# Gated linear attention on one core: the head norms' factors placed among the weight splits, the second scaling one unit later, the first scaled queries in other tiles

## The chip, the cores and the metric

The kernel runs on one core of one Trainium2 chip. The metric is the time of one execution on the device, in microseconds; the median of the runs shown counts. The kernel before takes 2088.75 us (median of 3 runs, 2087.92 to 2089.33).

## What is computed

One layer of a streaming encoder over 256 frames of width 2048, in float32: half a SwiGLU, a mixer, a cross attention over 256 memory tokens, another half SwiGLU, and a norm. The change lies in the mixer. One projection `W_in` gives a pool group, and queries, keys, values and an output gate for four heads of gated linear attention. Cut to what matters:

```python
qc = q * DK ** -0.5;  k_dec = k * exp(b_end - cum);  q_dec = qc * exp(b_end)
scores = einsum(qc, k_dec);  o = einsum(scores, v) + einsum(q_dec, state)   # chunks of 64 frames
o = o * rsqrt(mean(o * o, axis=-1) + 1e-6)        # a norm of its own for every head
o = o * head_norm * silu(g)                       # g: the output gate's projection
x = x + concat(y_pool, o) @ W_out
```

The kernel folds the decay between chunks into copies of the queries that are scaled by products of decays, one set per head: these are the scaled queries. The factor of a head norm is one number per frame and head.

## The kernel before, in words

**Weights and units.** The work is a stream of units. A unit is 1 MB of weights in a `raw` tile, loaded by SyncE, and the TensorE products that use it. For float32 accuracy ScalarE casts a rounded high part (`wh`, line 1621) and VectorE subtracts it to get the low part (`wl`, line 453); these two are the weights' parts. Some units save products by adding blocks first (a tile `T` at line 486, parts `xh` and `xl` at lines 279 and 280). There are three buffers each of `raw`, `wh` and `wl`, and parts are made up to two units ahead of the products.

**Order.** `st.op(f, after)` places a step `f` so many units later in the stream. What the program issues is then ordered, engine by engine, by a scheduler that works with a timeline of its own. Two helpers bind it: the parts of the weights follow one another on ScalarE and on VectorE (`in_turn`, line 257), and `among_weights` (line 270) places a step behind the parts issued so far on both engines and makes the next parts follow the last instruction that the step returns. A step outside these helpers goes where the scheduler finds room, instruction by instruction.

**The mixer.** The order of its blocks in `W_in` is: queries and keys, the low-rank gate, values, two pool blocks (`block_a`, products at line 347 into `pa`), the output gate (`block_s`, lines 362 and 507, into `pt`), with the pool map among it. The attention runs between these products. `decay` (line 1067) makes the decays `E` and their products `F`. `scores(h)` copies and scales the queries of head `h` (lines 1152 and 1154), multiplies them with the keys (line 1162) and moves the result to `ST` (line 1168). `attend` multiplies with the values (lines 1175 and 1178) and squares the result (line 1184). `head_norms(b)` does the following for heads 2b and 2b+1: it sums the squares on TensorE into `pn` (line 1197), takes the factor with `rsqrt` (lines 209 to 224: five VectorE instructions on 128x4 values with a ScalarE square root at line 215 behind the first), and makes four diagonal tiles from it (`diagonal`, line 228). `head_scale(b)` multiplies ones with the diagonals on TensorE (line 233, `ps`) to spread the factors, and multiplies the heads' output `oz` with them (line 1211). `gate` (line 1218) uses that result after the output gate's block.

The end of the attention falls into the second pool block, which has four units (parts `wh_6023`, `wh_6103` and `wh_6173` are its last three), and into the first units of the output gate (`wh_6231`, then the tile that holds `raw_6107`, then the unit of `raw_6177`, which adds blocks first).

Of the kernel before, what the change touches and what calls it, by code (L numbers as in the profile page):

```python
# [7 lines left out]
F32 = mybir.dt.float32  # L8
# [6 lines left out]
P = 128  # L15
# [5 lines left out]
NB = 512  # L21
# [3 lines left out]
DV = 256  # L25
# [74 lines left out]
def build(ctx, tc, I, out):  # L100
# [9 lines left out]
    scope = {"stack": None}  # L110
# [26 lines left out]
    def ptile(name):  # L137
        return psum.tile([P, 2, NB], F32, tag="ps", name=name)
# [6 lines left out]
    def uid(s):  # L145
        cnt[0] += 1
        return f"{s}{cnt[0]}"
# [61 lines left out]
    def rsqrt(dst, sums, n, w):  # L209

        v, r = chain[:, 0, :w], chain[:, 1, :w]
        nc.vector.tensor_scalar(
            out=v, in0=sums, scalar1=0.25 / n, scalar2=0.25 * EPS, op0=ALU.mult, op1=ALU.add
        )
        nc.scalar.activation(r, v, AF.Sqrt)
        nc.vector.reciprocal(out=dst, in_=r)
        if w == 1:
            nc.vector.tensor_scalar(
                out=v, in0=v, scalar1=dst, scalar2=r, op0=ALU.mult, op1=ALU.add
            )  # L220
        else:
            nc.vector.tensor_tensor(out=v, in0=v, in1=dst, op=ALU.mult)
            nc.vector.tensor_tensor(out=v, in0=v, in1=r, op=ALU.add)
        return nc.vector.reciprocal(out=dst, in_=v)

    def diagonal(col):
        d = scope["pool"].tile([P, P], F32, tag="diag", name=uid("diag"), bufs=4)
        nc.vector.tensor_scalar_mul(d, ident, col)
        return d
# [35 lines left out]
    def behind_weights(f):  # L265

        with tc.issue_after(latest["vector"].ins), tc.issue_after(latest["scalar"].ins):
            return f()

    def among_weights(f):  # L270


        scalar, vector = behind_weights(f)
        latest["vector"] = vector
        if scalar is not None:
            latest["scalar"] = scalar
# [682 lines left out]
    def mt(name, shape, tag=None, bufs=1):  # L959
        t = whole_lines(scope["pool"], shape, F32, tag or name, uid(name), bufs)  # L960
        mix[name] = t
        return t
# [12 lines left out]
    def m4():  # L975
        return scope["pool"].tile([P, 2 * 2 * (S + PAD)], F32, tag="m4", name=uid("m4"), bufs=3)
# [155 lines left out]
    def score_tile(h):  # L1132
        if h < 2:
            s = ctile() if h else mt("ST", [P, 2, S], "wa2")
        else:
            if h == 2:
                mix["two"] = scope["pool"].tile([P, 4 * NB], F32, tag="T", name=uid("ST"), bufs=1)
            s = mix["two"][:, (h - 2) * NB : (h - 1) * NB].rearrange("p (a b) -> p a b", a=2)
        mix["ST", h] = s
        nc.gpsimd.memset(s[64:128, 0, 0:CH], 0.0)  # L1140
        nc.gpsimd.memset(s[64:128, 1, 2 * CH : 3 * CH], 0.0)
        return s

    def scores(h):
        q, kd, E, F = mix["q"][:, h, :], mix["k"][:, h, :], mix["E"], mix["F"]
        e = lambda c: E[:, 4 * h + c : 4 * h + c + 1]
        f = lambda i: F[:, i, h : h + 1]
        QD = scope["pool"].tile([P, 3 * NB], F32, tag=("xh", "xl")[h % 2], name=uid("QD"), bufs=1)
        at = (0, 3 * CH, 5 * CH)
        factors = {(0, 1): e(1), (0, 2): f(0), (0, 3): f(2), (1, 2): e(2), (1, 3): f(1), (2, 3): e(3)}  # L1150
        for j in range(3):
            nc.scalar.copy(QD[:, at[j] + j * CH : at[j] + (j + 1) * CH], q[:, j * CH : (j + 1) * CH])
            for c in range(j + 1, 4):
                nc.vector.tensor_scalar_mul(
                    QD[:, at[j] + c * CH : at[j] + (c + 1) * CH], q[:, c * CH : (c + 1) * CH],
                    factors[j, c],
                )
        ps = ptile(uid("pq"))
        for j in range(4):
            part = slice((j % 2) * CH, (j % 2 + 1) * CH)  # L1160
            rhs = QD[:, at[j] + j * CH : at[j] + S] if j < 3 else q[:, 3 * CH :]
            nc.tensor.matmul(
                ps[part, j // 2, j * CH : S], kd[:, j * CH : (j + 1) * CH], rhs, start=True, stop=True
            )
        s = score_tile(h)
        for j in range(4):
            part = slice((j % 2) * CH, (j % 2 + 1) * CH)
            nc.vector.tensor_copy(s[part, j // 2, j * CH :], ps[part, j // 2, j * CH : S])
# [23 lines left out]
    def head_norms(b):  # L1192
        pn = ptile(uid("pn"))
        for i in range(2):
            sq = mix["osq", 2 * b + i]
            for t in range(2):
                nc.tensor.matmul(
                    pn[:, 0, 2 * i + t : 2 * i + t + 1], sq[:, 0, t * P : (t + 1) * P],
                    ones[:, 0:1], start=True, stop=True,
                )  # L1200
        r = mt("r", [P, 4])
        rsqrt(r, pn[:, 0, :4], DV, 4)
        mix["diag"] = [diagonal(r[:, i : i + 1]) for i in range(4)]

    def head_scale(b):
# [38 lines left out]
    for f, h, after in (  # L1244
        (scores, 0, 1), (scores, 1, 1), (scores, 2, 2), (scores, 3, 2), (head, 0, 3), (head, 1, 3),
        (head_norms, 0, 4), (head, 2, 4), (head_scale, 0, 5), (head, 3, 5), (head_norms, 1, 6),
        (head_scale, 1, 7),
    ):
        st.op(lambda f=f, h=h: f(h), after)
    block_a(wblock(w_in, 0), xs, ev_pool(0))  # L1250
# [166 lines left out]
    for b in range(2):  # L1417
# [3 lines left out]
        for j in (1, 0):  # L1421
            h = 2 * b + j
# [218 lines left out]
def program(shapes):  # L1641
    import concourse.bacc as _bacc

    nc = _bacc.Bacc("TRN2", target_bir_lowering=False, num_devices=1)
    args = {
        name: nc.dram_tensor(f"in_{name}", shapes[name], F32, kind="ExternalInput").ap()
        for name in _INS
    }
    out = nc.dram_tensor("out", _OUT, F32, kind="ExternalOutput").ap()
    with tile.TileContext(nc, schedule_with_timeline_sim=True) as tc, ExitStack() as ctx:  # L1650
        build(ctx, tc, args, out)
    return nc
# [10 lines left out]
```

## Time and profile before

| | us |
|---|---|
| median of 3 runs | 2088.75 |
| the profiled execution, by the clock of the runs | 2088.16 |
| its span, first to last instruction | 2086.4 |
| TensorE matmul busy | 2065.4 |
| VectorE busy | 1840.4 |
| ScalarE busy | 1157.2 |

The span leaves out 1.8 us that lie around it. A row of the timeline gives the start in us from the span's start, the duration in us, the engine (PE is TensorE, DVE VectorE, ACT ScalarE, SP SyncE), line, operation and tiles, how many instructions are merged in it, and in brackets the idle time before it with what ended that. Matmuls overlap, so a start-to-start distance says more than a duration. A row of the waits gives the total in us, the number of times and the longest. A row of the windows gives the busy time and count of each engine in a stretch, and PEclk, the share of the full TensorE clock that was granted.

### The profile page before, as it was taken

What the parts mean: (1) busy time and instruction counts of PE and PEld (TensorE: products, weight loads), DVE (VectorE), ACT (ScalarE), POOL (GpSimd) and SP (SyncE); (2) the same over time, 40 slices, a digit from 0 to 9 for tenths busy, and PEclk for the clock granted to TensorE, in tenths of its full rate; (3) what the DMA queues carried; (4) which work ended last, traced back from release to release, by engine and by line L of the source; (5) the groups of instructions that cost most, each with busy time, mean ns of one, the idle gap of its engine ahead of it and who ended that gap; (6) DMA issues with size and microseconds to landing.
All of it is one profiled execution on the core that took longest, in us unless ns stands there. A gap on an engine that the chain in (4) does not pass through costs nothing.

```text
span 2086.4 us, 24196 instructions
## 1 busy us (share of the span) xinstructions
PE 2065.4 (99%) x9531; PEld 1719.8 (82%) x9531; DVE 1840.4 (88%) x1745; ACT 1157.2 (55%) x1157; POOL 107.5 (5%) x98
## 2 busy tenths in 40 slices
PE   9999999999999999899999999999999999999998
PEld 7888888888888888788888888888888888888886
DVE  7998899989998768779888887889988999889987
ACT  7655455645554665365756544566554556545554
POOL 0000000000000000000001000000100010000001
PEclk9999999999999999999999999999999999999999
DMA  7666666567656655366855555666576765676664
GB/s 263 207 200 229 231 222 222 182 224 243 222 198 224 231 175 182 121 202 222 278 186 179 169 187 175 207 206 228 183 237 209 240 205 198 223 242 222 207 229 150
DMA packets 125034, 435.94 MB, mean 209 GB/s; under 512 B 9844, under 2 KB 13528, under 8 KB 124536
## 3 DMA queue, kind: packets, MB, share of 16 engines
q1 hardware_dynamic: 124744, 433.86, 61.6%
q8 instruction: 75, 1.23, 0.2%
q10 hardware_dynamic: 176, 0.53, 0.1%
q14 instruction: 39, 0.32, 0.0%
HBM read 417.58 MB, written 16.78 MB: 208 GB/s over the span
## 4 chain that ended last, share of the span: by engine, by line
PE 97%; DVE 1%; issue 0%; ACT 0%; DMA 0%; SPq 0%; DVEq 0%; ACTq 0%
PE pt L362 61%; PE pt L507 29%; PE pa L347 2%; PE ph L782 1%; PE pl L1357 1%; PE pv L1394 1%; DVE wl L453 0%; PE px L793 0%; PE pp L1027 0%; DMA x<-in_x 0%; PE pe L362 0%; ACT wh L1621 0%; PE pa L1054 0%; PE po L1175 0%; PE tm L1304 0%
## 5 line engine op out<-in xcount | busy, mean ns | idle before, releaser
L362 PE MATMUL pt<-wh,xs 128*128 128x512 f32 x2368 | 761.4, 391 | 0.3 <-ACT xs L236 0.3
L453 DVE TENSOR_TENSOR wl<-raw,wh 128x2048 fp32r<-128x2048 f32 (+1 forms) x245 | 521.5, 2136 | 100.3 <-ACT wh L1621 100.0
L1621 ACT CAST wh<-raw 128x2048 fp32r<-128x2048 f32 x245 | 467.6, 1912 | 244.4 <-PE pt L362 122.0
L362 PEld LDWEIGHTS pt<-wh,xs 128*128 128x128 f32 x2368 | 444.9, 188 | 92.2 <-ACT xs L236 0.5
L489 ACT CAST wh<-T 128x1024 fp32r<-128x1024 f32 x258 | 270.6, 1054 | 377.5 <-DVE T L486 363.4
L362 PE MATMUL pt<-wl,xs 128*128 128x512 f32 x1184 | 462.5, 391 | 0.0
L362 PE MATMUL pt<-wh,ys 128*128 128x512 f32 x1440 | 454.8, 389 | 0.0
L362 PEld LDWEIGHTS pt<-wh,ys 128*128 128x128 f32 x1440 | 270.2, 188 | 55.6
L453 DVE TENSOR_TENSOR wl<-T,wh 128x2048 fp32r<-128x2048 f32 (+1 forms) x129 | 289.8, 2246 | 3.0 <-ACT wh L489 2.4
L362 PE MATMUL pt<-wl,ys 128*128 128x512 f32 x720 | 280.8, 390 | 0.6 <-DVE wl L453 0.6
L362 PEld LDWEIGHTS pt<-wl,xs 128*128 128x128 f32 x1184 | 222.9, 188 | 45.4 <-DVE wl L280 0.2
L280 DVE TENSOR_TENSOR xl<-raw,xh 128x1536 fp32r<-128x1536 f32 x129 | 225.8, 1751 | 17.8 <-ACT xh L279 17.7
L279 ACT CAST xh<-raw 128x1536 fp32r<-128x1536 f32 x129 | 190.9, 1480 | 65.8 <-PE pt L507 43.4
L486 DVE TENSOR_TENSOR T<-T,raw 128x512 f32<-128x512 f32 x258 | 177.9, 690 | 6.7
L362 PEld LDWEIGHTS pt<-wl,ys 128*128 128x128 f32 x720 | 135.2, 188 | 28.9 <-DVE wl L453 1.0
L457 POOL TENSOR_TENSOR wl<-raw,wh 128x768 fp32r<-128x768 f32 x46 | 85.4, 1857 | 1421.0 <-DVE wl L453 1394.8
L486 DVE TENSOR_TENSOR T<-raw 128x1024 f32<-128x1024 f32 x129 | 157.0, 1217 | 0.5
L507 PE MATMUL pt<-wh,xs 128*128 128x512 f32 x388 | 150.8, 389 | 0.0
L507 PE MATMUL pt<-xh,xs 128*128 128x512 f32 x400 | 149.1, 389 | 0.0
L507 PE MATMUL pt<-wh,xe 128*128 128x512 f32 x320 | 124.3, 389 | 0.0
L507 PEld LDWEIGHTS pt<-xh,xs 128*128 128x128 f32 x400 | 75.1, 188 | 15.6
L507 PEld LDWEIGHTS pt<-wh,xs 128*128 128x128 f32 x388 | 72.8, 188 | 15.1
(257 smaller groups left out, 2184.9 us busy)
## 6 DMA issues: line engine op xcount, KB each, us to landing
raw<-in_ffn_w_down SPq DMA_DIRECT2D x88, 1024.0 KB, 5.4
raw<-in_ffn_w_up SPq DMA_DIRECT2D x80, 1024.0 KB, 5.0
raw<-in_ffn_w_gate SPq DMA_DIRECT2D x77, 1024.0 KB, 5.1
raw<-in_w_in SPq DMA_DIRECT2D x32, 1024.0 KB, 5.1
raw<-in_xattn_w_kv SPq DMA_DIRECT2D x32, 1024.0 KB, 5.0
raw<-in_w_out SPq DMA_DIRECT2D x16, 1024.0 KB, 5.6
raw<-in_xattn_w_q SPq DMA_DIRECT2D x16, 1024.0 KB, 5.7
raw<-in_xattn_w_o SPq DMA_DIRECT2D x16, 1024.0 KB, 5.7
```

The costliest lines, as they stand in the source:

```text
L279: in_turn("scalar", lambda: nc.scalar.copy(hi, src))
L280: in_turn("vector", lambda: nc.vector.tensor_tensor(out=lo, in0=src, in1=f32(hi), op=ALU.subtract))
L347: nc.tensor.matmul(o, w, x, start=k == 0 and i == 0, stop=last and i == 1)
L362: nc.tensor.matmul(ps, a, w, start=first and i == 0, stop=last and i == 2)
L453: in_turn("vector", lambda: nc.vector.tensor_tensor(out=lo[:, :n], in0=src[:, :n], in1=f32(hi[:, :n]), op=ALU.subtract))
L457: rest = nc.gpsimd.tensor_tensor(out=lo[:, n:], in0=src[:, n:], in1=f32(hi[:, n:]), op=ALU.subtract)
L486: in_turn("vector", lambda: nc.vector.tensor_tensor(out=o, in0=a, in1=b, op=ALU.add))
L489: in_turn("scalar", lambda: nc.scalar.copy(th[:, c], t[:, c]))
L507: nc.tensor.matmul(banks[n], x, w, start=n in fresh and j == 0, stop=n in ends and j == 2)
L782: nc.tensor.transpose(v[:, i, h * P : (h + 1) * P], g[:, h, i * P : (i + 1) * P], ident)
L1357: nc.tensor.matmul(ps[:, t, :M], ys[:, 4 * h + d, a, tok], xa["K", h][:, d, b, :], start=i == 0, stop=i == 11,)
L1621: in_turn("scalar", lambda: nc.scalar.copy(hi, raw))
```

## The change

Three edits, all in the mixer:

```diff
 def scores(h):
-        QD = scope["pool"].tile([P, 3 * NB], F32, tag=("xh", "xl")[h % 2], name=uid("QD"), bufs=1)
+        QD = m4() if h < 2 else scope["pool"].tile(
+            [P, 3 * NB], F32, tag=("xh", "xl")[h % 2], name=uid("QD"), bufs=1
+        )
...
 def head_norms(b):
         r = mt("r", [P, 4])
-        rsqrt(r, pn[:, 0, :4], DV, 4)
+        among_weights(lambda: (None, rsqrt(r, pn[:, 0, :4], DV, 4)))
...
         (head_norms, 0, 4), (head, 2, 4), (head_scale, 0, 5), (head, 3, 5), (head_norms, 1, 6),
-        (head_scale, 1, 7),
+        (head_scale, 1, 8),
```

The scaled queries of heads 0 and 1 get tiles of the tag `m4` (three buffers, used by the decay and the pool blocks) and no longer the `xh` and `xl` tiles that the parts of the weights use. The factor's steps become one group among the weights' parts; the diagonals stay outside it. The scaling of the second pair is issued one unit later. From line 1149 on, line numbers grow by two.

**VectorE at the end of the second pool block, before.** `pn_6211` holds the sums of squares of the second pair, `r_6216` its factor, `diag_6223` the first of its diagonals; line 212, which reads `pn_6211`, stands three rows above the first one shown.

```order
L216 RECIPROCAL r_6216<-chain 128x4
L486 TENSOR_TENSOR T_6329<-T_6329,raw_6177 128x512
L280 TENSOR_TENSOR xl_6333<-raw_6177,xh_6332 128x1536
L323 TENSOR_TENSOR m_6314<-m_6314,R_5413 128x2x256
L222 TENSOR_TENSOR chain<-chain,r_6216 128x4
L453 TENSOR_TENSOR wl_6331<-T_6329,wh_6330 128x2048
L997 TENSOR_TENSOR m_6315<-m_6314 128x2x271
L223 TENSOR_TENSOR chain<-chain 128x4
L997 TENSOR_TENSOR m_6316<-m_6315 128x2x269
L224 RECIPROCAL r_6216<-chain 128x4
L997 TENSOR_TENSOR m_6315<-m_6316 128x2x265
L228 TENSOR_SCALAR diag_6223<-ident,r_6216 128x128
```

The factor's small steps stand between sums, parts of weights and the pool's windows. The parts `wl_6232` and `wl_6277` of the gate's first two units stand ahead of all of this.

The same place after the change, from the last head's output on:

```order
L1192 TENSOR_TENSOR t_6155<-t_6155 128x256
L212 TENSOR_SCALAR chain<-pn_6211 128x4
L216 RECIPROCAL r_6216<-chain 128x4
L222 TENSOR_TENSOR chain<-chain,r_6216 128x4
L223 TENSOR_TENSOR chain<-chain 128x4
L224 RECIPROCAL r_6216<-chain 128x4
L453 TENSOR_TENSOR wl_6232<-raw_6026,wh_6231 128x2048
L453 TENSOR_TENSOR wl_6270<-raw_6107,wh_6269 128x2048
L486 TENSOR_TENSOR T_6329<-raw_6177 128x1024
L228 TENSOR_SCALAR diag_6223<-ident,r_6216 128x128
```

The five steps now follow one another; the parts of the gate's first two units and one sum have moved from ahead of them to between the factor and its diagonals.

On ScalarE at that place, after the change (`wh_6269` is the high part that was `wh_6276`; `c_6318` and `c_6374` are copies out of the pool block's accumulators):

```order
L1186 ACTIVATE t_6155<-po_6150 128x512
L1623 CAST wh_6269<-raw_6107 128x2048
L279 CAST xh_6332<-raw_6177 128x1536
L215 ACTIVATE chain<-chain 128x4
L318 COPY c_6318<-pa_6109 128x512
L318 COPY c_6374<-pa_6110 128x512
```

Before, the square root at line 215 stood one row lower, behind the copy `c_6318`; it is still behind both casts.

**TensorE at the same place, after the change.**

```order
L347 MATMUL pa_6110<-xs,wl_6174 128x256
L347 MATMUL pa_6110<-xs,wh_6173 128x512
L233 MATMUL ps_6307<-diag_6223,ones 128x128
L362 MATMUL pt_6344<-wh_6231,xs 128x512
L362 MATMUL pt_6344<-wl_6232,xs 128x512
```

Although the scaling is issued a unit later, the first of its four spreads stays between the pool block's last product and the gate's first one, as before, and the other three stay sixteen matmuls later. The second matmul into `pn_6211` (from `t_6155`) has moved from the middle of the block's last unit to the end of the unit before.

**VectorE at the first scaled queries** (`m_5840` and `m_5862` are the tiles of heads 0 and 1, `T_5662` and `xl_5666` belong to the unit of `raw_5538`, one of the last of the values' block), as a piece of the difference:

```order
 L1101 TENSOR_TENSOR F_5589<-E_5584 128x4
+L1156 TENSOR_SCALAR m_5840<-q_5523,E_5584 128x64 x3
 L486 TENSOR_TENSOR T_5662<-T_5662,raw_5538 128x512
+L1156 TENSOR_SCALAR m_5862<-q_5523,E_5584 128x64 x2
 L1102 TENSOR_TENSOR F_5589<-F_5589,E_5584 128x4
+L1156 TENSOR_SCALAR m_5840<-q_5523,F_5589 128x64 x2
+L1156 TENSOR_SCALAR m_5862<-q_5523,F_5589 128x64 x2
+L1156 TENSOR_SCALAR m_5862<-q_5523,E_5584 128x64
```

With two more, twelve scalings move ahead of the last low parts of the values' block (`xl_5666`, `wl_5664`, `wl_5701`); on ScalarE their six copies move ahead of `xh_5665` and `wh_5663` in the same way. The scalings of heads 2 and 3 take the room in which those of heads 0 and 1 stood, and leave theirs in the first pool block.

## The prediction

> **What bounds the kernel now.** I read the page first: the busy times and the chain that ended last.
>
> ```profile
> span 2086.4 us, 24196 instructions
> PE 2065.4 (99%) x9531; PEld 1719.8 (82%) x9531; DVE 1840.4 (88%) x1745; ACT 1157.2 (55%) x1157; POOL 107.5 (5%) x98
> PE 97%; DVE 1%; issue 0%; ACT 0%; DMA 0%; SPq 0%; DVEq 0%; ACTq 0%
> ```
>
> TensorE is busy for 99% of the span and is 97% of the chain. The change adds no product and takes none away, so it can only touch the time in which TensorE stands still or runs slowly. The waits of TensorE, the second view, say how much that is.
>
> ```profile
> PE ps L233 <- DVE diag L228: 8.3, 1, 8.3
> PE pwarm L206 <- POOL ident masks.py:199: 1.4, 1, 1.4
> PE px L719 <- DMA x<-in_x: 1.0, 1, 1.0
> PE pt L362 <- DVE wl L453: 0.6, 1, 0.6
> ```
>
> One wait is worth more than all the others together: the first spread of a head norm's factor waits 8.3 us for its diagonal. The timeline of TensorE puts it at the end of the second pool block, so it is the second pair's (the view counts one wait, so the first pair's had none).
>
> ```profile
> 857.62 0.39 PE L347 MATMUL pa<-xs,wh 128*128 128x512 f32 x1
> 866.35 0.77 PE L233 MATMUL ps<-diag,ones 128*128 128x128 f32 x2 [8.34 <-DVE diag L228]
> ```
>
> The last pool product ends at 858.0 and the spread starts at 866.35. The wait also has an aftermath, which the windows show, on the columns PE busy (count) and PEclk.
>
> ```profile
> core 0: us, PE busy (x) PEld busy (x) DVE busy (x) ACT busy (x) POOL busy (x), PEclk, DMA share, GB/s
> 858.00:861.00 3.00, 0.01 (x1) 0.00 (x0) 3.00 (x6) 2.52 (x4) 0.00 (x0) 1.00 0.79 306
> 861.10:866.30 5.20, 0.00 (x0) 0.00 (x0) 5.20 (x10) 0.00 (x0) 0.14 (x1) 0.50 0.61 203
> 866.40:871.20 4.80, 4.80 (x13) 3.83 (x14) 4.63 (x11) 0.62 (x1) 0.00 (x0) 0.50 0.00 0
> 871.40:876.20 4.80, 4.80 (x25) 4.01 (x25) 3.67 (x7) 1.42 (x2) 0.00 (x0) 1.00 0.00 0
> ```
>
> About 3 us into the wait the granted clock falls to one half, and it stays there for some 4.8 us of work: 13 matmuls where the next 4.80 us hold 25. That costs 12/25 of 4.80, or 2.3 us. Wait and aftermath together are 10.6 us, 0.5% of the time, and no edit here can win more.
>
> **The factor's chain, step by step.** Before, VectorE was late because other work stood between the steps of the factor.
>
> ```profile
> 853.88 2.29 DVE L453 TENSOR_TENSOR wl<-raw,wh 128x2048 fp32r<-128x2048 f32 x1 [3.61 <-ACT wh L1621]
> 856.10 1.22 DVE L486 TENSOR_TENSOR T<-raw 128x1024 f32<-128x1024 f32 x1
> 857.23 0.15 DVE L212 TENSOR_SCALAR chain<-pn 128x4 f32<-128x4 f32 x1
> ...
> 858.59 0.17 DVE L216 RECIPROCAL r<-chain 128x4 f32<-128x4 f32 x1
> ...
> 861.52 0.15 DVE L222 TENSOR_TENSOR chain<-chain,r 128x4 f32<-128x4 f32 x1
> ...
> 864.43 0.15 DVE L223 TENSOR_TENSOR chain<-chain 128x4 f32<-128x4 f32 x1
> ...
> 865.18 0.17 DVE L224 RECIPROCAL r<-chain 128x4 f32<-128x4 f32 x1
> ...
> 865.92 0.87 DVE L228 TENSOR_SCALAR diag<-ident,r 128x128 f32<-128x128 f32 x4
> ```
>
> From line 212 to the diagonals it took 8.7 us for under 1 us of work on the factor. In the new order VectorE comes to line 212 earlier: the parts `wl_6232` and the second gate unit's no longer precede it. What ends last is then the square root, which stands on ScalarE behind two casts.
>
> ```profile
> 851.94 1.91 ACT L1621 CAST wh<-raw 128x2048 fp32r<-128x2048 f32 x1 [4.72 <-PE pa L347]
> 853.76 1.47 ACT L279 CAST xh<-raw 128x1536 fp32r<-128x1536 f32 x1
> ...
> 857.84 0.21 ACT L215 ACTIVATE chain<-chain 128x4 f32<-128x4 f32 x1
> ```
>
> The first cast starts when TensorE frees a buffer of `wh`, at the end of the unit of `wh_6103`; nothing moves that by much. The second ends at 853.76 + 1.47 = 855.2, and the square root at 855.4. The sums `pn_6211` are there by then: their matmuls move from the middle of the block's last unit to the end of the unit that frees the buffer, so to about 852. Four steps follow (lines 216 to 224): 0.17 + 0.15 + 0.15 + 0.17 = 0.64, with small gaps 0.7, so 856.1. Now comes what the change puts **behind** the factor and ahead of its diagonals: two low parts of 2.2 us (856.10 - 853.88 from start to start) and one sum of 1.1 us (857.23 - 856.10), 5.5 us in all: 861.6. Before, the spread began 0.43 us after the diagonals did (866.35 against 865.92), so now at about **862.1**. The wait shrinks from 8.3 to some 4.1 us; it does not go. Moving the scaling by a unit buys nothing by itself, since the scheduler left the first spread between the same two products. Gain: 866.35 - 862.1 = **4.25 us**.
>
> The parts that now queue behind the factor are needed when the gate's first unit starts, behind the same spread; they end before the diagonals do, so they add nothing. Nor does the load behind the second cast:
>
> ```profile
> 843.25 0.37 SPq L629 DMA_DIRECT2D raw<-in_w_in  x1
> ```
>
> ```profile
> raw<-in_w_in SPq DMA_DIRECT2D x32, 1024.0 KB, 5.1
> ```
>
> That load of `raw_6177` is issued when `wl_6174` frees a buffer and lands 5.1 us later, at 848.4. `wl_6174` now stands behind one more part, `wl_6104`, 2.2 us: landing at 850.6, still 3.1 us before the cast at 853.76. The loads that wait for the two moved parts are issued up to 10 us later than before, the first at about 858; the next cast that reads one began at 875.40, so they are covered.
>
> ```profile
> 875.40 1.91 ACT L1621 CAST wh<-raw 128x2048 fp32r<-128x2048 f32 x1 [1.46 <-PE pt L362]
> ```
>
>
> **What it costs earlier.** Twelve scalings and six copies move ahead of the last parts of the values' block.
>
> ```profile
> 788.18 1.76 DVE L280 TENSOR_TENSOR xl<-raw,xh 128x1536 fp32r<-128x1536 f32 x1
> 790.09 2.29 DVE L453 TENSOR_TENSOR wl<-T,wh 128x2048 fp32r<-128x2048 f32 x1
> 792.30 2.28 DVE L453 TENSOR_TENSOR wl<-raw,wh 128x2048 fp32r<-128x2048 f32 x1
> 798.50 0.24 DVE L1154 TENSOR_SCALAR QD<-q,E 128x64 f32<-128x64 f32 x1
> 798.66 0.24 DVE L1154 TENSOR_SCALAR QD<-q,F 128x64 f32<-128x64 f32 x1
> 793.57 0.99 ACT L1152 COPY QD<-q 128x64 f32<-128x64 f32 x6
> 792.04 0.39 PE L507 MATMUL pt<-xl,xs 128*128 128x512 f32 x1
> 794.08 0.39 PE L507 MATMUL pt<-wl,ys 128*128 128x512 f32 x1
> 796.35 0.39 PE L362 MATMUL pt<-wl,xs 128*128 128x512 f32 x1
> ```
>
> A scaling takes 0.16 us from start to start (798.66 - 798.50), twelve take 1.95 us. The three parts end at 789.94, 792.38 and 794.58, and TensorE first reads them at 792.04, 794.08 and 796.35: slack of 2.1, 1.7 and 1.8 us. So VectorE comes late by about **0.25 us**, once. The casts are further ahead, and the copies' 0.99 us hide there. Ends: 0, if the small scalings pack better, and 1.95 + 0.99 - 1.7 = 1.25 us, if the copies delay the same parts as well. The twelve scalings that leave the first pool block win nothing, since TensorE waited for nothing there.
>
> **The half clock.** The new wait is half as long, and whether the clock still falls decides over 2.3 us. The two rows to weigh: above, the clock was still full 3.0 us after the last product had ended; at the kernel's end it was still full at 2079.6 and half from 2079.7.
>
> ```profile
> 2076.88 0.39 PE L362 MATMUL pt<-wh,ys 128*128 128x512 f32 x1
> ```
>
> ```profile
> 2077.30:2079.60 2.30, 0.00 (x0) 0.00 (x0) 1.82 (x6) 1.42 (x6) 0.36 (x1) 1.00 0.32 111
> 2079.70:2086.30 6.60, 0.00 (x0) 0.00 (x0) 2.02 (x5) 1.33 (x2) 0.00 (x0) 0.50 0.64 233
> ```
>
> There it fell 2.4 us after the last product (2077.27). So the time to the fall is not fixed; 2.4 and 3.1 us were enough, and 4.1 us probably are too. I leave the aftermath in the sum as it was, at 2.3 us. [...]
>
> **The sum**, against the profiled execution: 2088.16 - 4.25 + 0.25 = 2084.2. The median of the runs shown lies 0.6 us above that execution, and the aftermath's length will vary by more than that; I take **2084.4** for the median after.
>
> **Rivals.**
> 1. *The clock does not fall.* [...] For it: the clock stood at 1.00 for 3.0 us of the old wait. Against it: the fall after 2.4 us at the end. Time: 2084.2 - 2.3 = 2081.9.
> 2. *The early queue becomes a wait*: the scalings and copies delay the values' parts by their upper bound of 1.25 us. For it: slack of 1.7 us against 1.95. Time: 2088.16 - 4.25 + 1.25 = 2085.2.
> 3. *The change does not do what it says*: the diagonals stay as late, because the parts ahead of them fill the room that the factor's steps left (they are 5.5 of the 8.7 us). For it: the spread has not moved on TensorE. Against it: the square root has a fixed place on ScalarE, 2.4 us earlier. Time: 2088.2 to 2088.7.
> 4. *Slower: the square root waits a unit more.* It stands behind the cast of `wh_6269`. If that cast's buffer comes free only with the pool block's last product (858.0 instead of 851.9), all behind it starts 6.0 us later: spread at 868.1, 1.75 us later than before, with the early 0.25 some 2090.2. It decides from a delay of 4.25 us on. Against it: before, the same cast in the same rotation of three buffers began at 851.94, in the middle of the wait for that block.
>
> **How the numbers follow.** Forecast 62% (2083.4 to 2085.4), rival 1 17%, rival 2 8%, rival 3 7%, rival 4 with anything worse 6%. About 0.2%, 4.2 us, is what a measurement of this kernel can tell from no change; that is 2084.57, and my forecast lies on it. Some 60% of its chance lies below (0.37), with rival 1 that makes 0.54 for faster; the rest of the forecast, rivals 2 and 3 make 0.41; rival 4 reaches over 0.2% only if the clock's aftermath grows with it and VectorE slips too, and with what I don't see I give slower 0.05. The range goes from rival 1 to beyond rival 2: 2081.9 to 2086.4.
>
> **What would show it.** One wait of `ps` for `diag` of 4 to 4.5 us, a square root at line 215 directly behind the `xh` cast, line 224 some 0.7 us later, two low parts and a sum before line 228, and a stretch of about 5 us at a clock of 0.50 behind the spread, or none (rival 1). A wait for `wl` or `xl` of a few tenths near 794 would be the early cost. I am wrong if the wait is as long as before, if it is gone, or if another wait of over 1 us appears in the mixer.

## The result, and the profile after

The changed kernel takes **2083.67 us** (median of 13 runs, 2082.77 to 2085.64) against 2088.1 us for the kernel before (13 runs, 2086.91 to 2089.33) on the same chip: ratio 0.9979, 95% interval 0.9971 to 0.9988. That is 4.4 us faster. The profiled execution took 2083.59 us. Its page, the span and the busy times:

```profile
span 2081.8 us, 24192 instructions
PE 2066.2 (99%) x9531; PEld 1720.6 (83%) x9531; DVE 1839.2 (88%) x1745; ACT 1157.2 (56%) x1157; POOL 107.5 (5%) x98
```

The busy times have not changed by as much as 0.1%. The waits of TensorE, in us in total, times and longest:

```profile
PE ps L233 <- DVE diag L228: 3.9, 1, 3.9
PE pwarm L206 <- POOL ident masks.py:199: 1.4, 1, 1.4
PE pt L362 <- DVE wl L453: 0.6, 1, 0.6
PE pa L347 <- DVE v L575: 0.3, 1, 0.3
```

The wait of the first spread has gone from 8.3 to 3.9 us, 4.4 us and thus the size of the result. A new wait of 0.3 us belongs to the early cost. The wait for `x` at the program's start (1.0 us before) is not in this execution; over the executions shown below it is anything from 0 to 1.8 us, whatever the kernel.

The factor's chain on ScalarE (the square root is line 215):

```profile
851.72 1.91 ACT L1623 CAST wh<-raw 128x2048 fp32r<-128x2048 f32 x1 [4.53 <-PE pa L347]
853.53 1.47 ACT L279 CAST xh<-raw 128x1536 fp32r<-128x1536 f32 x1
854.90 0.20 ACT L215 ACTIVATE chain<-chain 128x4 f32<-128x4 f32 x1
```

and on VectorE:

```profile
852.01 0.16 DVE L212 TENSOR_SCALAR chain<-pn 128x4 f32<-128x4 f32 x1 [3.77 <-PE pn L1199]
855.13 0.18 DVE L216 RECIPROCAL r<-chain 128x4 f32<-128x4 f32 x1 [2.96 <-ACT chain L215]
...
855.74 0.18 DVE L224 RECIPROCAL r<-chain 128x4 f32<-128x4 f32 x1
855.84 4.46 DVE L453 TENSOR_TENSOR wl<-raw,wh 128x2048 fp32r<-128x2048 f32 x2
860.22 1.22 DVE L486 TENSOR_TENSOR T<-raw 128x1024 f32<-128x1024 f32 x1
861.35 0.87 DVE L228 TENSOR_SCALAR diag<-ident,r 128x128 f32<-128x128 f32 x4
```

Two stretches make up the delay. VectorE stands still for 2.96 us between lines 212 and 216, because the square root stands behind two casts. Then 5.5 us of parts and sum (855.84 to 861.35) stand between the factor and its diagonals. TensorE meanwhile:

```profile
857.45 0.39 PE L347 MATMUL pa<-xs,wh 128*128 128x512 f32 x1
861.78 0.77 PE L233 MATMUL ps<-diag,ones 128*128 128x128 f32 x2 [3.94 <-DVE diag L228]
```

The windows around the wait (the second column of numbers is PE busy and its count, PEclk the granted clock):

```profile
core 0: us, PE busy (x) PEld busy (x) DVE busy (x) ACT busy (x) POOL busy (x), PEclk, DMA share, GB/s
857.90:859.90 2.00, 0.00 (x0) 0.00 (x0) 2.00 (x2) 0.56 (x1) 0.00 (x0) 1.00 0.36 55
860.20:861.70 1.50, 0.00 (x0) 0.00 (x0) 1.50 (x4) 0.18 (x1) 0.00 (x0) 0.50 0.98 385
861.80:866.80 5.00, 5.00 (x13) 4.03 (x14) 5.00 (x9) 1.81 (x2) 0.00 (x0) 0.50 0.64 263
866.90:871.90 5.00, 5.00 (x26) 4.19 (x26) 4.96 (x8) 0.10 (x1) 0.12 (x1) 1.00 0.64 210
```

The clock falls all the same, between 859.9 and 860.2, and stays at one half until about 866.85: 13 matmuls in 5.00 us where the next 5.00 us hold 26, so 2.5 us lost, as before.

### The profile page after: what moved, and what is told of

Same layout as the page of the kernel before. It is cut to its first block, busy times and chain, and to the rows that moved or that the text cites. A ratio compares the mean times of both kernels' runs of the same rounds, so it can differ in the third digit from the quotient of the medians.

```text
span 2081.8 us, 24192 instructions
## 1 busy us (share of the span) xinstructions
PE 2066.2 (99%) x9531; PEld 1720.6 (83%) x9531; DVE 1839.2 (88%) x1745; ACT 1157.2 (56%) x1157; POOL 107.5 (5%) x98
## 4 chain that ended last, share of the span: by engine, by line
PE 96%; DVE 2%; ACT 1%; issue 1%; DVEq 0%; POOL 0%; ACTq 0%; POOLq 0%
PE pt L362 61%; PE pt L507 29%; PE pa L347 2%; PE ph L782 1%; DVE wl L453 1%; PE pl L1359 1%; PE pv L1396 1%; PE px L793 0%; PE pp L1027 0%; PE pe L362 0%; DVE T L486 0%; PE px L719 0%; ACT wh L489 0%; PE pwarm L206 0%; PE pa L1054 0%
```

## The experiments

The theory: the grouped factor carries the whole gain by shortening one wait; the late square root and the parts ahead of the diagonals are what is left of it; the half clock is a second cost that comes with the idle time. The rivals: the edits work only together; the later scaling or the moved queries make the room; the half clock has a cause of its own. All ratios are against the kernel before on the same chip (2087.7 us for the three edits taken alone and for the diagonals inside the group, 2088.4 for the others).

### The factor's group alone

```diff
-        rsqrt(r, pn[:, 0, :4], DV, 4)
+        among_weights(lambda: (None, rsqrt(r, pn[:, 0, :4], DV, 4)))
```

> The kernel before with one edit alone: the factor's five steps as one group among the weights' parts. My theory (this edit carries the whole result): TensorE's wait of the first spread for its diagonal falls from 8.3 us to 3.9 as in the changed kernel, the clock still falls to one half behind it, and the time is 4.4 us below before, about 2083.7. Rival (the three edits work together, the later scaling or the moved queries make the room): the wait stays above 6 us and the time above 2086.

Measured: 2083.36 us, ratio 0.998 (0.9971 to 0.9989). The first of its waits is that of the changed kernel:

```profile
PE ps L233 <- DVE diag L228: 3.9, 1, 3.9
```

This edit alone gives the whole result. The half clock is there too, but shorter; its windows:

```profile
859.00:861.80 2.80, 0.00 (x0) 0.00 (x0) 2.80 (x2) 0.06 (x1) 0.00 (x0) 1.00 0.68 199
862.40:865.20 2.80, 2.80 (x8) 2.32 (x9) 2.80 (x8) 0.76 (x1) 0.00 (x0) 0.50 1.02 418
865.50:868.30 2.80, 2.80 (x16) 2.39 (x15) 2.80 (x3) 0.81 (x1) 0.00 (x0) 1.00 0.22 32
```

With the same wait of 3.94 us as in the changed kernel, the clock was low for some 3.4 us and not 6.8.

### The later scaling alone, and the moved queries alone

```diff
-        (head_scale, 1, 7),
+        (head_scale, 1, 8),
```

> The kernel before with one edit alone: the second pair's scaling issued one unit later. My theory: the spread keeps its place between the pool block's last product and the gate's first, the wait stays at 8.3 us, the time at 2088.1 within 0.4. Rival (the later unit is what brings the factor forward): the wait falls by 2 us or more, time 2086 or less.

Measured: 2088.62 us, ratio 1.0005 (0.9996 to 1.0013); the wait is 8.3 us, as before. The later unit does nothing by itself.

```diff
-        QD = scope["pool"].tile([P, 3 * NB], F32, tag=("xh", "xl")[h % 2], name=uid("QD"), bufs=1)
+        QD = m4() if h < 2 else scope["pool"].tile(
+            [P, 3 * NB], F32, tag=("xh", "xl")[h % 2], name=uid("QD"), bufs=1
+        )
```

> The kernel before with one edit alone: the scaled queries of heads 0 and 1 in the m4 tiles. My theory: the wait at the spread stays 8.3 us; one short wait of 0.3 us appears at the first pool product near 801, and the time rises by 0.2 to 0.4 us, at the edge of what can be told: 2088.1 to 2088.6. Rival (the scalings and copies delay the values' parts in full): 1.25 us, 2089.4. Rival (the queries make the room at the spread): wait shorter than 8 us, time under 2087.

Measured: 2088.27 us, ratio 1.0 (0.9991 to 1.0008). Two of its waits:

```profile
PE ps L233 <- DVE diag L228: 8.3, 1, 8.3
...
PE pa L347 <- DVE v L575: 0.2, 1, 0.2
```

The queries bring the short wait and leave the long one. A cost of a few tenths is too little to show in the time.

### The scaled queries of all heads moved

```diff
-        QD = scope["pool"].tile([P, 3 * NB], F32, tag=("xh", "xl")[h % 2], name=uid("QD"), bufs=1)
+        QD = m4() if h < 4 else scope["pool"].tile(
...
```

> The kernel before with the scaled queries of all four heads in m4 tiles. 18 scalings instead of 12 stand ahead of the last low parts of the values' block, and the twelve that stood ahead of VectorE's first sum of that block's results (line 575) are gone. My theory (the early cost is whatever VectorE is late by at the next thing that TensorE waits for): the wait for line 575 disappears, and one for wl or xl of 0.5 to 1 us stands near 790 to 796 in its place. Rival (the cost comes from the tiles, not from the order on VectorE): the wait for line 575 stays at 0.2 to 0.5 us.

Measured, in a single execution: 2088.84 us, which by itself says nothing of a change of this size. The wait for line 575 is gone, and one for a low part has come. TensorE's row:

```profile
794.77 0.50 PE L507 MATMUL pt<-wl,ys 128*128 128x512 f32 x1 [0.79 <-DVE wl L453]
```

The wait has moved to where the order on VectorE has changed, as it would not if the tiles themselves were the cost: what counts here is how late VectorE is at the next thing that TensorE needs.

### The diagonals inside the group

```diff
-        rsqrt(r, pn[:, 0, :4], DV, 4)
-        mix["diag"] = [diagonal(r[:, i : i + 1]) for i in range(4)]
+        def factor():
+            rsqrt(r, pn[:, 0, :4], DV, 4)
+            mix["diag"] = []
+            for i in range(4):
+                d = scope["pool"].tile([P, P], F32, tag="diag", name=uid("diag"), bufs=4)
+                last = nc.vector.tensor_scalar_mul(d, ident, r[:, i : i + 1])
+                mix["diag"].append(d)
+            return None, last
+        among_weights(factor)
```

This is the changed kernel with one more edit; the cast of `wh` is line 1632 in it and the diagonals are line 1210.

> The changed kernel with the four diagonals inside the group, so that they follow the factor at once and the two low parts and the sum come behind them. My theory (what is left of the wait is those parts and the sum, and the half clock is its aftermath): the diagonals are made at 856.1, before the pool block's last product ends at 857.8; the wait of 3.9 us goes and with it the half clock (5.1 us at half speed, 2.5 us of work): 6.4 us less than the changed kernel, 2077.2; if the gate's first low part, which now ends near 859.1, is asked for at 858.5, a wait of 0.6 us takes its place: 2077.8. Rival 1 (the half clock comes for another reason): only 3.9 us less, 2079.7, with a stretch at clock 0.50 still there. Rival 2 (the parts behind the group become the wait): a wait of over 3 us for a low part, 2081 or more.

Measured: 2078.5 us, ratio 0.9957 (0.9943 to 0.997). The wait for the diagonal is gone, and with it the half clock behind it: 851 to 891 us run at a PEclk of 1.00. The time is 1.3 us above my 2077.2. A wait that I did not foresee has come in later, in the output gate's block:

```profile
PE pt L362 <- DVE v L589: 1.1, 1, 1.1
```

It stands in place of a wait of 0.6 us for a low part that the kernel has both before and after the change, so it explains only about half a us. From the last pool product to the kernel's last product, the start and the end of the program left out, this run takes 1209.2 us and the changed kernel 1214.9: 5.7 us less, of the 6.4 that I had put down. What makes up the rest of the 1.3 us is open.

And the mechanism was not quite the one that I wrote. The square root moved as well; ScalarE:

```profile
852.02 0.20 ACT L215 ACTIVATE chain<-chain 128x4 f32<-128x4 f32 x1 [3.64 <-DVE chain L212]
852.92 1.92 ACT L1632 CAST wh<-raw 128x2048 fp32r<-128x2048 f32 x1 [0.70 <-PE pa L347]
854.74 1.48 ACT L279 CAST xh<-raw 128x1536 fp32r<-128x1536 f32 x1
```

It now stands ahead of both casts, so the diagonals are made at 853.1 (I had 856.1). This run alone doesn't tell whether the square root or the parts behind the factor made the wait. The next one does.

### The square root early, the two parts still ahead of the diagonals

```diff
+    def diagonals():
+        mix["diag"] = []
+        for i in range(4):
+            d = scope["pool"].tile([P, P], F32, tag="diag", name=uid("diag"), bufs=4)
+            last = nc.vector.tensor_scalar_mul(d, ident, mix["r"][:, i : i + 1])
+            mix["diag"].append(d)
+        return None, last
...
-        (head_norms, 0, 4), (head, 2, 4), (head_scale, 0, 5), (head, 3, 5), (head_norms, 1, 6),
-        (head_scale, 1, 7),
+        (head_norms, 0, 4), (diagonals, 0, 4), (head, 2, 4), (head_scale, 0, 5), (head, 3, 5),
+        (head_norms, 1, 6), (diagonals, 1, 8), (head_scale, 1, 8),
...
-        st.op(lambda f=f, h=h: f(h), after)
+        st.op(lambda f=f, h=h: among_weights(f) if f is diagonals else f(h), after)
```

`head_norms` has the factor's group here and keeps the factor in `mix["r"]`; the queries are as before the change.

> The kernel before with the factor as one group, the later scaling, and the diagonals as a group of their own two units after the factor: the two low parts stay between factor and diagonals, the sum does not, and the square root stands ahead of the two casts on ScalarE, as it also did in the run with the diagonals inside the group (there it ended at 852.2 and not at 855.1). My theory, mended after that run (the late square root is 3 us of the wait that is left, the parts alone are hidden): the factor is ready at 853.1, two low parts take 4.4, diagonals at 857.5, and the pool block ends at 857.8 to 858.6: no wait for a diagonal, no half clock, 2078.0 to 2078.5. Rival (the parts between factor and diagonals are the cause wherever the square root stands): a wait of 2.8 us (3.9 less the sum's 1.1), 2080.5 without and 2082.5 with a half clock.

Measured: 2078.19 us, ratio 0.9952 (0.9938 to 0.9965), no wait for a diagonal. VectorE:

```profile
851.88 0.18 DVE L216 RECIPROCAL r<-chain 128x4 f32<-128x4 f32 x1 [0.33 <-ACT chain L215]
...
852.48 0.18 DVE L224 RECIPROCAL r<-chain 128x4 f32<-128x4 f32 x1
852.58 4.46 DVE L453 TENSOR_TENSOR wl<-raw,wh 128x2048 fp32r<-128x2048 f32 x2
856.96 0.86 DVE L1209 TENSOR_SCALAR diag<-ident,r 128x128 f32<-128x128 f32 x4
```

The idle time ahead of line 216 is 0.33 us where the changed kernel has 2.96, and the same two low parts, 4.4 us, still fit between factor and diagonals: TensorE goes from the pool block to the spread at 858.10 without a wait. So in the changed kernel the late square root and the parts behind the factor make the wait **together**: taking away the first leaves room for the two parts. Two things were not run. Whether the sum would fit as well: by these rows it would end at 856.96 + 1.14 = 858.1, and the wait would be a few tenths. And whether a late square root with the diagonals directly behind the factor would do: by the changed kernel's rows they would begin at 855.84, and the spread could start some 0.4 us later, ahead of the last pool product's end at 857.84. Both are estimates. The wait of 1.1 us for line 589 stands in this run too.

### The wait filled with spare products

```diff
+        if b:
+            x = xs[:, 0].rearrange("p a b -> p (a b)")
+            with tc.issue_after(latest["pa"].ins):
+                for _ in range(14):
+                    fill = nc.tensor.matmul(ps[:, 0, :], xs[:, 0, 0, :P], x, start=True, stop=True)
+            with tc.issue_after(fill.ins):
+                latest["spread"] = nc.tensor.matmul(
+                    ps[:, 0, :P], ones, mix["diag"][0], start=True, stop=True
+                )
+        for i in range(b, 4):
```

`latest["pa"]` is the pool block's last product, and the gate's products are bound behind the first spread, so that the order on TensorE stays.

> The changed kernel with 14 spare products of 0.23 us (their results are overwritten by the spreads) between the pool block's last product and the first spread, 3.3 us that fill most of the wait of 3.9 us; the spread still waits for its diagonal. My theory (the stretch at clock 0.50 is the aftermath of TensorE standing idle, a cost of its own beside the wait): the diagonal comes as late as before, a wait of 0.5 to 1.1 us is left, the clock stays at 1.00, and the time falls by the 2.5 us of work that the half clock cost: 2081.2. Rival (the half clock has another cause, or idling of over 0.5 us is enough): the stretch at 0.50 stays and the time is that of the changed kernel, 2083.7.

Measured: 2081.64 us, ratio 0.9969 (0.9957 to 0.998), 2.0 us less than the changed kernel. A wait of 0.65 us for the diagonal is left, and the diagonal itself comes as late (the spread starts at 861.82). Its windows:

```profile
857.90:861.10 3.20, 3.20 (x15) 2.36 (x13) 3.20 (x3) 0.60 (x2) 0.00 (x0) 1.00 0.52 133
862.30:867.00 4.70, 4.70 (x26) 3.96 (x25) 4.70 (x8) 1.46 (x2) 0.00 (x0) 1.00 0.62 250
```

26 matmuls fit into 4.70 us behind the spread, at a clock of 1.00. All six runs (2081.36 to 2082.6 us) lie below all thirteen of the changed kernel (from 2082.77). Useless work in the wait makes this kernel 2.0 us faster: with TensorE busy in most of the wait the clock stayed at 1.00, so the half clock of the changed kernel came with standing idle and cost time on top of its wait of 3.94 us.

### The spread two units later

```diff
-        (head_scale, 1, 7),
+        (head_scale, 1, 9),
```

This is the kernel before with that one number.

> The kernel before with one number changed: the second pair's scaling issued two units later instead of one. The spreads then stand behind the gate's third unit on TensorE, near 880, while the factor stays as spread out as before (diagonals at about 866). My theory (the wait depends on the spread's place as much as on the factor; one unit more did not move it past the boundary, two do): no wait for a diagonal, no half clock, 8.3 + 2.3 us less than before, 2077.4. Rival (without the wait VectorE is late with what follows, since it was 99% busy from 858 to 866): waits for low parts of several us in the gate's first units, 2081 or more.

Measured: **2077.57 us**, ratio 0.9948 (0.9936 to 0.9961): 10.8 us faster than before by the medians, more than the changed kernel gains, whose interval ends at 0.9971. By its median it is the fastest version, though the intervals don't tell it from the two with the square root early. All its waits of TensorE:

```profile
PE pwarm L206 <- POOL ident masks.py:199: 1.4, 1, 1.4
PE pt L362 <- DVE wl L453: 0.6, 1, 0.6
PE px L719 <- DMA x<-in_x: 0.2, 1, 0.2
PE pt L507 <- DVE xl L280: 0.2, 1, 0.2
```

The last step of the factor and the diagonals on VectorE, and the four spreads on TensorE:

```profile
864.60 0.17 DVE L224 RECIPROCAL r<-chain 128x4 f32<-128x4 f32 x1
...
865.35 0.87 DVE L228 TENSOR_SCALAR diag<-ident,r 128x128 f32<-128x128 f32 x4
```

```profile
870.67 1.05 PE L233 MATMUL ps<-diag,ones 128*128 128x128 f32 x8
```

The factor is as spread out and as late as before, and nobody waits for it, since TensorE asks for it 5 us after the first diagonal is there. I had expected the spreads near 880; they stand at 870.67, far enough behind the diagonals all the same. No wait for a part of the weights has come in its place.

## Why the prediction was right, point by point

**The one wait.** Right: the change touched the wait that the views gave as worth more than all the others. The group alone gave the result, the later scaling alone nothing. One sentence was a little too strong: that no edit here can win more than 10.6 us. The half clock before lasted to 871.3, 4.95 us of work, so wait and aftermath are 8.3 + 2.5 = 10.8 us, and 10.8 is what the spread two units later gained.

**The chain.** Right in its order and nearly in its times. The square root was put at 855.4 and ended at 855.1; line 224 at 856.1, ended at 855.9; two parts and a sum at 5.5 us, took 5.5; the spread at 862.1, started at 861.78. The wait was put at some 4.1 and is 3.94 us, the gain at 4.25 and is 4.40.

**The later scaling buys nothing.** Right by the run with that edit alone. The spread must get past the boundary between two blocks, and one unit does not take it there; two do, and then the whole wait goes.

**The early cost.** Right in size, partly by luck, and wrong in place. I put 0.25 us on low parts near 794. They came just in time, ending 0.1 to 0.2 us before TensorE's first product with each, and TensorE waited 0.26 us for line 575, VectorE's first sum of the values' results. This is that line before the change, and the first pool product:

```profile
799.47 0.68 DVE L575 TENSOR_TENSOR v<-pt,v 128x512 f32<-128x512 f32 x1
801.33 0.39 PE L347 MATMUL pa<-xs,wh 128*128 128x512 f32 x1
```

and both after:

```profile
800.58 0.68 DVE L575 TENSOR_TENSOR v<-pt,v 128x512 f32<-128x512 f32 x1
801.32 0.50 PE L347 MATMUL pa<-xs,wh 128*128 128x512 f32 x1 [0.26 <-DVE v L575]
```

VectorE was 1.1 us later there by the clock of the execution. TensorE would have been 0.3 us earlier (801.06 without the wait, against 801.33), so VectorE lost 1.4 us against it, on a slack of 1.1. I compared the delay with the slack of the next three parts and should have followed it to the next point at which VectorE catches up.

The distances from start to start tell more than the wait. From a product ahead of these low parts (785.47 before, 784.90 after) to the second pool product (801.56 and 801.65) the changed kernel takes 0.66 us longer. In the first pool block it gets 0.34 us back, between the first score product of head 2 and the first product with the values (7.54 us before, 814.35 to 821.89; 7.20 after, 814.44 to 821.64): the score products of heads 2 and 3 now form one group there, where before they were two groups with pool products between them. The run with the queries' edit alone agrees: from VectorE's line 1100 (785.75) to the second pool product (802.42) it takes 16.67 us, as the changed kernel does, against 16.03 before, and from there to the last pool product 55.72 against 56.06. So my sentence that the first pool block wins nothing was wrong, the cost ahead of it is over twice what I wrote, and the net of 0.3 us agrees with my 0.25 because the two errors nearly cancel.

**The half clock.** Right that it came, and near in size (2.3 us in the sum, 2.5 in the profiled execution), but partly by luck. I argued that 2.4 and 3.1 us of standing idle had been enough, so 4.1 probably would be. In the run with the moved queries the clock held for 5.3 us, longer than the whole wait here; and with the group alone, the same wait cost 1.5 us behind it and not 2.5. Neither the fall nor its size was as sure as my sum took them. Rival 1 gave the price of losing the half clock as 2.3 us; filling the wait gained 2.0. The 17% that I gave rival 1 was my estimate, and no run shows it. In both executions with a wait of 3.94 us the clock fell: in the changed kernel at most 2.4 us after the last product (857.84 to 860.2), with the group alone 3.6 us after it (858.43 to 862.0).

**Rivals 2 to 4.** None came. The queries' edit alone brought a wait of 0.2 us and a net cost of 0.3, not 1.25; the diagonals moved by 4.6 us (865.92 to 861.35); the first of the two casts ahead of the square root began at 851.72 (851.94 before), so its buffer came free a unit ahead of the pool block's last product, as before.

**The sum.** 2084.2 against the profiled 2083.59, 2084.4 against the median of 2083.67. The wait accounts for 0.15 of that; the wait for `x` at the start, 1.0 us before and none here, is in no term. The start of the program differs from execution to execution, so the sum over the whole doesn't close to better than about half a us. Without the start it does better: from the last pool product to the kernel's last product it is 1219.26 us before (857.62 to 2076.88) and 1214.85 after (857.45 to 2072.30), 4.41 us less, which is what the wait has lost.

## What to carry to other kernels

Where one engine is busy for 99%, the few us that are left have an address: find the one wait, then ask of both sides whether the producer can come earlier **or the consumer ask later**; here one number on the consumer's side was worth 10.8 us, the regrouping on the producer's 4.3. A group that keeps small steps together helps only as far as it binds every engine of the chain and holds the last step, the one that is waited for: here the square root on ScalarE and the diagonals were left outside it. Price a stall together with the slow clock that a run shows behind it: here 1.5 to 2.5 us behind a wait of 3.94.

## What the runs showed of the hardware

In these runs the half clock is not proportional to the wait. With a wait of 3.94 us it lasted 6.8 us in the changed kernel (860.05 to 866.85) and 3.4 in the run with the factor's group alone (862.0 to 865.4); with 8.3 us, 10.2 us in the kernel before (861.05 to 871.3) and 6.8 in the run with the moved queries (863.8 to 870.6). The windows of that run, whose last product ended at 858.5:

```profile
859.00:863.60 4.60, 0.00 (x0) 0.00 (x0) 4.60 (x7) 2.10 (x3) 0.00 (x0) 1.00 0.67 224
863.90:866.80 2.90, 0.00 (x0) 0.00 (x0) 2.90 (x8) 0.00 (x0) 0.14 (x1) 0.50 0.68 277
866.90:870.50 3.60, 3.60 (x10) 2.92 (x11) 3.50 (x9) 0.62 (x1) 0.00 (x0) 0.50 0.00 0
870.70:874.30 3.60, 3.60 (x20) 3.04 (x20) 3.46 (x6) 0.45 (x1) 0.00 (x0) 1.00 0.00 0
```

Here the clock stayed full for over 5 us of idle time, in the changed kernel for only 2 to 2.4. No run shows what decides when it falls and how long it stays low.

The same wait then costs 1.5 us behind it in one execution (half of the 3.0 us from the spread, at 862.4 in the run with the group alone, to 865.4) and 2.5 in another. The price shows in the time: from the last pool product to the kernel's last product the run with the group alone takes 1213.94 us, 0.9 us less than the changed kernel, though the wait is the same. Each of these lengths is read from one execution; how much they differ between executions of one kernel was not measured.
